# Batch norm over a matrix product on one core: the first block of w is loaded ahead of the first rows of x

## The chip, the cores and the metric

The kernel runs on one core of a Trainium2 chip. The metric is device time in microseconds, the median of several runs. Engines are named as in the profile: PE is TensorE (PEld its weight loads), DVE is VectorE, ACT is ScalarE, POOL is GpSimd, SP is SyncE. POOL and SP here also issue DMAs.

## The reference

```python
batch, m, k, n = 16, 512, 1024, 768
# x (16, 512, 1024), weight (1024, 768), float32; gamma ones, beta zeros
y = np.matmul(x, weight)
mean = np.mean(y, axis=(0, 1), keepdims=True)
var = np.var(y, axis=(0, 1), keepdims=True)
y_norm = (y - mean) / np.sqrt(var + eps)
return (gamma * y_norm + beta).astype(np.float32)
```

The product has 8192 rows and 768 columns. Mean and variance of each column go over all 8192 rows, so nothing can be stored before the last row has been multiplied.

## The kernel before

x is worked through in 16 chunks of 512 rows. The loads convert x and w to bfloat16 on the way into SBUF. x is needed with its k index across the partitions, so every landed piece of x goes through a transpose on DVE (L413, L420) before PE can use it; w needs nothing more. The k index is cut into four blocks called jw, each of 256 values: `w_sb[:, jw]` is one block of w, and a product of 512 rows and 128 columns sums over jw = 0 to 3 and two halves e.

**Loads.** `load_x` (L385) issues four DMAs for a piece of x, `load_w` (L377) four for one or more blocks of w, all on POOL's queue. The list `order` (L425) names the loads in turn: `("x", q)` is a piece of 256 rows, called x0, x1, x2, x3 in this text, `("w", a, b)` the blocks a to b-1 of w, called w0 for block 0, w1 for block 1, and w2 for blocks 2 and 3 together; `("c", c)` is a chunk of 512 rows and `("p", ...)` a part of the last chunk. POOL's queue has at most eight loads out at one time: each further one waits for the one issued eight before it. Ahead of all this SP reads one element of each of 128 rows of w into the tile `touched` (L341 to L344), which nothing uses afterwards.

**PE's start.** `wake` (L569) issues products of zeros into a bank nobody reads: first WAKE = 8 of 512 columns in float32 and SMALL = 22 small ones, and later FILL = 2 more of the large ones (L764). Then come the first chunk's products. `part(0, 1, [0])` is x0 with block 0 of w (four products L492 for the first 256 columns, eight L557 for the other 512), `part(1, 2, [0])` is x1 with block 0, `part(0, 2, [1])` both with block 1, and the rest takes blocks 2 and 3. After that each chunk of 512 rows is multiplied with the first 256 columns (L492, through `rows_unit`) and, for the first chunks, with the other columns (L557, through `col_unit`).

**What sets the order.** The kernel is written as tasks with an engine, a cost, dependencies and a priority. `arrange` (L122) plays them through with modelled times and writes down the order in which each engine issues them; each engine then runs its list strictly in that order, waiting on semaphores for data. The FILL task depends in the plan on w0's load alone:

```python
part(0, 1, [0])
fill_slot = Slot(banks)
pe_task(0.87 * FILL, wake(FILL, fill_slot), [w_ready[0]], takes=[fill_slot])
part(1, 2, [0])
part(0, 2, [1])
```

On the chip it waits for nothing of w. All products write into a ring of eight PSUM banks (`psum`), FILL among them.

The tail of the kernel (normalising and storing, L920 onwards, and L1279 to L1295 for the last columns) isn't touched.

Of the kernel before, what the change touches and what calls it, by code (L numbers as in the profile page):

```python
# [227 lines left out]
def kernel(  # L228
# [9 lines left out]
    nc = tc.nc  # L238
    f32 = mybir.dt.float32
# [8 lines left out]
    P = 128  # L248
# [9 lines left out]
    WAKE = 8  # L258
    FILL = 2
    SMALL = 22  # L260
    EARLY = 4
    SHORT = 2
    GA = 2
# [5 lines left out]
    RC = C - 2  # L269
    XT, YB, SQ = C - EARLY, 27, 3  # L270
    ADDED = (0,6,16,28,40)
# [10 lines left out]
    singles = ctx.enter_context(tc.tile_pool(name="singles", bufs=1))  # L282
# [7 lines left out]
    def seq(bi):  # L290

        ins = bi.ins
        prev = last.get(ins.engine)
        if prev is not None:
            tc.add_manual_dep(
                ins, prev,
                mybir.DependencyInfo(mybir.DependencyClass.NoSync, mybir.DependencyReason.DATA),
                reason="order",
            )
        last[ins.engine] = ins.name  # L300
        return bi
# [36 lines left out]
    warm = singles.tile([P, 1], f32)  # L338

    seq(nc.scalar.activation(warm, eps_sb, AF.Sqrt))  # L340
    touched = singles.tile([P, 1], f32)  # L341
    first_rows = weight.rearrange("(i jw c e) n -> i jw c (e n)", i=4, jw=JW, e=2)
    for i in range(4):
        seq(nc.sync.dma_start(touched[32 * i:32 * i + 32], first_rows[i, 0, :, 0:1]))  # L344


    tasks, turns = [], {}
# [11 lines left out]
    def act(occ):  # L359
        return {"ACT": (occ, occ + 0.11)}  # L360
# [61 lines left out]

    for c in range(C):
        x_slot[c] = Slot(xts)
    order = [("x", 0), ("w", 0, 1), ("x", 1), ("w", 1, 2), ("w", 2, 4)]  # L425
    order += [("x", q) for q in range(2, SHORT * QPC)] + [("c", c) for c in range(SHORT, C - 1)]
    at = M - CH
    for rows in (CH-P,P):
# [81 lines left out]
    def part_chunk(c, now, engines, small=False, step=0.0, after=()):  # L510

        src = x_slot[c]
        slots = [Slot(sqs if jw < SQ else ys) for jw in range(JW)] if small else [Slot(xts)] * JW
        ts = []

        def copy(jw):
            def emit(eng):
                if small:
                    if jw < SQ:
                        x_pl = sqpool.tile([P, 2, CH], bf16, tag="sq")  # L520
                    else:
                        x_pl = ypool.tile([P, 2, CH], bf16, tag="y")
                    slots[jw].tile = [x_pl]
                elif jw == 0:
                    x_pl = xtpool.tile([P, JW, 2, CH], bf16, tag="xT")
                    slots[0].tile = [x_pl[:, i] for i in range(JW)]
                dst = slots[jw].tile[0 if small else jw]
                pairs = src.tile[:, jw].rearrange("p m e -> p e m")
                seq(nc.scalar.copy(dst, pairs) if eng == "ACT" else ENG[eng].tensor_copy(dst, pairs))  # L529
            return emit  # L530

        for jw in range(JW):
            new = small or jw == 0
            ts.append(task(
                now + step * jw, engines, copy(jw), [x_ready[c, q, JW] for q in range(QPC)] + list(after) + ([] if new else ts[:1]),
                len(engines) > 1, uses=[src] + ([] if new else [slots[jw]]), takes=[slots[jw]] if new else []))
        plain[c] = slots, ts, small
# [31 lines left out]
    def wake(count, slot):  # L569
        def emit(eng):  # L570
# [3 lines left out]
            small = idle_sb[:, 0:P // 2].bitcast(bf16)  # L574
            for _ in range(SMALL if count == WAKE else 0):
                seq(nc.tensor.matmul(idle_ps[:, 0:P], small, small, start=True, stop=True))  # L576
# [244 lines left out]
    for c in range(1, RC):  # L821
        for ts in ([0, 1], [2, 3]):
            rows_unit(c, ts)
        if c in PARTED:
            part_chunk(c, clock[0] + (4.0 if c < EARLY else 20.0), act(1.05))
        columns = ([c - 1] if 0 < c - 1 < EARLY and c - 1 in PARTED else []) + (
            [c] if c < EARLY and c not in PARTED else [])
        for c1 in columns:
# [372 lines left out]
    STEP = {2: 1.9, 3: 2.3, 4: 2.3}  # L1201
    CHUNKS = {nt: list(range(EARLY, C)) for nt in range(GA, NT)}
    if LATE:
        late = [c for c in range(EARLY, C) if c in LATE or c + 1 - c % 2 * 2 in LATE]
        rest = [c for c in range(EARLY, C) if c not in late]
# [97 lines left out]
    order = arrange(tasks, turns)  # L1303
# [39 lines left out]
```

## Time and profile before

| | |
|---|---|
| median of 5 runs | 208.31 us (207.90 to 208.97) |
| the profiled execution | 208.15 us |
| its span, first to last instruction | 206.3 us |
| mean granted TensorE clock over the span | 0.979 |
| HBM read, written | 36.71 MB, 25.17 MB |
| loads on POOL's queue | 64.9% of the 16 DMA engines' span |

The span is what the profile's rows are measured in; 1.85 us of the execution lie outside it. The table in slices divides the span into 40 parts of 5.16 us. In the timeline a row gives start, length, engine, line, operation, the tile written and the tile read, the number of instructions merged in it, and in brackets the idle time of that engine before it and who ended it. In the chain of waits a row gives start, length, engine and line of the work that the end of the kernel depended on. A DMA's row shows its issue on POOL, not its transfer; the time from the start of an issue to its landing comes from the view of one source line.

### The profile page before, as it was taken

The page shows a single profiled execution, that of the slowest core. Times are in us where ns is not written, and L with a number is a line of the kernel's source. Part 1 is how long each engine was busy: PE and PEld are TensorE (multiplying, and loading weights), DVE is VectorE, ACT ScalarE, POOL GpSimd, SP SyncE. Part 2 cuts the span into 40 slices and gives each one's busy share as a digit, 9 for nine tenths or more (in the row PEclk, how much of TensorE's full clock was granted, in tenths as well). Part 3 has the DMA queues.
Part 4 walks back from the last instruction along what each step waited for, and adds up shares of the span by engine and source line. Part 5 has one row for each costly group of instructions (what it writes and reads, how often), then busy time and mean ns, then how long its engine had stood idle before and what let it go on. Part 6 is the DMA issues. An engine that isn't in the chain of part 4 may idle for free.

```text
span 206.3 us, 3516 instructions
## 1 busy us (share of the span) xinstructions
PE 192.5 (93%) x1226; PEld 117.9 (57%) x1226; DVE 156.4 (76%) x238; ACT 139.2 (67%) x248; POOL 131.7 (64%) x148
## 2 busy tenths in 40 slices
PE   7999999999999999999999999999999999996900
PEld 3467564747488888777865444444444445464900
DVE  4220879999999999968979998878999649666900
ACT  2000560369979999998859767997476777685960
POOL 7987954878498999998304998599945440800000
PEclk9999999999999999999999999999999999999695
DMA  5999999999999999999576998999999999999898
GB/s 60 173 185 192 195 196 196 199 194 196 191 193 196 197 197 196 196 197 194 93 99 205 330 341 300 259 354 275 321 301 250 302 299 314 313 344 347 254 347 255
DMA packets 98497, 48.73 MB, mean 236 GB/s; under 512 B 24240, under 2 KB 97968, under 8 KB 98480
## 3 DMA queue, kind: packets, MB, share of 16 engines
q0 software_dynamic: 34688, 18.36, 64.9%
q1 hardware_dynamic: 63792, 30.16, 53.9%
q8 instruction: 9, 0.15, 0.3%
q14 instruction: 8, 0.07, 0.1%
HBM read 36.71 MB, written 25.17 MB: 300 GB/s over the span
## 4 chain that ended last, share of the span: by engine, by line
PE 86%; ACT 6%; DMA 2%; DVE 1%; ACTq 0%; issue 0%
PE y_ps L557 52%; PE y_ps L492 24%; PE idle_ps L573 6%; ACT o_sb L1292 3%; PE o_ps L1027 2%; DMA r_sb<-y_sb 2%; PE a_ps L886 1%; ACT x_pl L529 1%; PE y_ps L735 1%; ACT y_sb L702 1%; PE idle_ps L576 1%; ACT y_ps L706 1%; ACT y_sb L810 1%; PE o_ps L1057 0%; ACT y_sb L654 0%; ACTq L1338 0%
## 5 line engine op out<-in xcount | busy, mean ns | idle before, releaser
L557 PEld LDWEIGHTS <-w_sb 128*128 128x128 bf16 x512 | 49.6, 97 | 57.3
L557 PE MATMUL y_ps<-x_pl,w_sb 128*128 128x512 bf16 x264 | 60.5, 379 | 0.0
L557 PE MATMUL y_ps<-xT_sb,w_sb 128*128 128x512 bf16 (+1 forms) x248 | 55.9, 377 | 0.0
L391 POOL DMA_DIRECT2D ring<-in_x_dram x76 | 47.5, 630 | 12.6 <-DVE xT_sb L413 4.9
L492 PE MATMUL y_ps<-w_sb,xT_sb 128*128 128x256 bf16 x448 | 50.6, 273 | 0.0
L492 PEld LDWEIGHTS <-xT_sb 128*128 128x128 bf16 x448 | 43.7, 98 | 7.3 <-issue 0.6
L420 DVE STREAM_TRANSPOSE xT_sb<-ring 128x1024 f32<-128x1024 f32 (+1 forms) x29 | 31.2, 1111 | 11.6 <-DMA ring<-in_x_dram 11.4
L693 DVE BATCH_NORM_STATS2 stats<-y_ps 128x6 f32<-128x512 f32 x46 | 30.7, 687 | 11.0 <-PE y_ps L557 10.9
L697 ACT CAST y_sb<-y_ps 128x512 bf16<-128x512 f32 x51 | 29.1, 591 | 13.1 <-DVE stats L693 11.4
L925 POOL TENSOR_TENSOR ring<-ring,sum 128x1024 f32<-128x1024 f32 (+1 forms) x11 | 23.7, 2182 | 14.8 <-DVE ring L920 14.8
L648 POOL TENSOR_TENSOR sum<-sum,sq_sb 128x512 f32<-128x512 f32 x21 | 26.9, 1280 | 3.3 <-ACT sq_sb L641 2.1
L641 ACT ACTIVATE sq_sb<-y_ps 128x512 f32<-128x512 f32 x28 | 16.3, 607 | 17.7 <-PE y_ps L492 17.2
L644 DVE TENSOR_TENSOR sum<-y_ps,sum 128x512 f32<-128x512 f32 x28 | 18.9, 675 | 9.2 <-ACT sq_sb L641 8.0
L529 ACT COPY x_pl<-xT_sb 128x1024 bf16<-128x1024 bf16 x24 | 24.4, 1051 | 1.7 <-DVE xT_sb L420 1.7
L529 POOL COPY x_pl<-xT_sb 128x1024 bf16<-128x1024 bf16 x15 | 16.1, 1109 | 8.0 <-DVE x_pl L529 5.2
L654 ACT CAST y_sb<-y_ps 128x512 bf16<-128x512 f32 x28 | 15.9, 600 | 7.7 <-DVE sum L644 7.4
L1192 ACT CAST ring<-ring 128x1024 f32<-128x1024 bf16 x15 | 15.7, 1048 | 2.7 <-DMA ring<-y_sb 2.5
L920 DVE TENSOR_TENSOR ring<-y_sb,a_ps 128x1024 f32<-128x1024 bf16 (+1 forms) x16 | 16.7, 1080 | 0.6 <-DMA out_dram<-ring 0.6
L1138 POOL TENSOR_TENSOR ring<-ring,sum 128x1024 f32<-128x1024 f32 x4 | 9.4, 2355 | 8.0 <-DVE ring L1134 8.0
L1027 PE MATMUL o_ps<-ident,y_sb 128*128 128x128 bf16 x104 | 11.9, 247 | 2.0 <-DVE y_sb L1279 2.0
L413 DVE STREAM_TRANSPOSE xT_sb<-ring 128x2048 bf16<-128x2048 bf16 x6 | 13.5, 2289 | 0.2 <-DMA ring<-in_x_dram 0.2
L573 PE MATMUL idle_ps<-idle_sb 128*128 128x512 f32 x20 | 11.5, 735 | 1.5 <-DVE idle_sb L313 1.5
(97 smaller groups left out, 156.2 us busy)
## 6 DMA issues: line engine op xcount, KB each, us to landing
out_dram<-ring SPq DMA_DIRECT2D x38, 512.0 KB, 4.0
ring<-in_x_dram POOLq DMA_DIRECT2D x52, 256.0 KB, 8.9
out_dram<-o_sb SPq DMA_DIRECT2D x6, 512.0 KB, 4.4
ring<-in_x_dram POOLq DMA_DIRECT2D x16, 128.0 KB, 5.2
out_dram<-ring SPq DMA_DIRECT2D x4, 256.0 KB, 2.7
w_sb<-in_weight_dram POOLq DMA_DIRECT2D x8, 96.0 KB, 4.5
w_sb<-in_weight_dram POOLq DMA_DIRECT2D x4, 192.0 KB, 5.3
ring<-in_x_dram POOLq DMA_DIRECT2D x4, 192.0 KB, 8.2
```

The source lines that it names most:

```text
L391: bi = seq(nc.gpsimd.dma_start(x_bf[32 * i:32 * i + 32], src[:, :, KQ * i:KQ * (i + 1)]))
L420: seq(nc.vector.transpose(dst, src[:, :, jw0:jw1]))
L492: seq(nc.tensor.matmul(y_ps[:, s], x_of(c, jw, e, t * P, (t + 1) * P), w_sb[:, jw, e, 0:NA], start=(s == 0 and jw == 0 and e == 0), stop=( ...
L529: seq(nc.scalar.copy(dst, pairs) if eng == "ACT" else ENG[eng].tensor_copy(dst, pairs))
L557: seq(nc.tensor.matmul(y_ps, w_sb[:, jw, e, nt * P:(nt + 1) * P], moving(c, jw, e, q0 * QR, q1 * QR, parted), start=(jw == 0 and e == 0 an ...
L573: seq(nc.tensor.matmul(idle_ps, idle_sb[:, 0:P], idle_sb, start=True, stop=True))
L644: seq(nc.vector.tensor_add(sum1, slot.tile[:, 0:n], sum1))
L648: seq(ENG[eng].tensor_add(acc, acc, state["sq"][:, 0:n]))
L693: seq(nc.vector.bn_stats(dst, slot.tile))
L697: seq(nc.scalar.copy(y(nt, c), slot.tile))
L920: seq(nc.vector.tensor_mul(slot.o, y_row[c].y[:, s0:s1], aff[0][:, None, :].to_broadcast([P, n, NA])))
L925: seq(ENG[eng].tensor_add(slot.o, slot.o, row[:, None, :].to_broadcast([P, n, NA])))
```

## The change

In the list `order`, `("w", 0, 1)` is put ahead of `("x", 0)`; the rest of the list stays. The length of the SP reads gets a name, TOUCH, with the value that stood there, 1.

```diff
@@ -258,6 +258,7 @@
+    TOUCH = 1
@@ -338,10 +339,10 @@
-    touched = singles.tile([P, 1], f32)
+    touched = singles.tile([P, TOUCH], f32)
     first_rows = weight.rearrange("(i jw c e) n -> i jw c (e n)", i=4, jw=JW, e=2)
     for i in range(4):
-        seq(nc.sync.dma_start(touched[32 * i:32 * i + 32], first_rows[i, 0, :, 0:1]))
+        seq(nc.sync.dma_start(touched[32 * i:32 * i + 32], first_rows[i, 0, :, 0:TOUCH]))
@@ -422,7 +423,7 @@
-    order = [("x", 0), ("w", 0, 1), ("x", 1), ("w", 1, 2), ("w", 2, 4)]
+    order = [("w", 0, 1), ("x", 0)] + [("x", 1), ("w", 1, 2), ("w", 2, 4)]
```

Two engines' instruction lists differ from before. POOL issues the four loads of w0 and then the four of x0, where it was the other way round. On PE the two idle products of FILL stand ahead of the first chunk's first products, where they stood between x0's and x1's products with block 0. DVE, ACT and SP issue the same instructions in the same order; DVE's first transpose still waits for x0.

## The prediction

> **What bounds the kernel now.** I read the page first (shares, then the slices), then TensorE's waits, then the chain of waits in order of time, then the timeline of the first 28 us on all engines, because the change touches only what is loaded there.
>
> ```profile
> PE 192.5 (93%) x1226; PEld 117.9 (57%) x1226; DVE 156.4 (76%) x238; ACT 139.2 (67%) x248; POOL 131.7 (64%) x148
> ...
> PE   7999999999999999999999999999999999996900
> ...
> DMA  5999999999999999999576998999999999999898
> ```
>
> TensorE is busy for 93% of the span, and in the first half the DMA engines are as full as it is. So a load that comes late has nowhere to hide unless TensorE doesn't need it yet. TensorE's own waits, all of the execution:
>
> ```profile
> PE o_ps L1027 <- DVE y_sb L1279: 2.0, 1, 2.0
> PE idle_ps L573 <- DVE idle_sb L313: 1.5, 1, 1.5
> PE a_ps L886 <- ACT y_sb L810: 0.2, 1, 0.2
> ```
>
> The columns are total, times and longest. It idles at the start, in the tail, and for 0.2 us in the middle; no wait names a load. The chain of waits (start, length) says what fills the start:
>
> ```profile
> 1.49 9.67 PE idle_ps L573 x16
> 11.16 1.23 PE idle_ps L576 x22
> 12.39 0.44 PE y_ps L492 x4
> 12.82 0.91 PE y_ps L557 x8
> 13.73 1.72 PE idle_ps L573 x4
> 15.45 0.44 PE y_ps L492 x4
> ...
> 19.47 1.75 PE y_ps L492 x16
> ...
> 24.83 3.57 PE y_ps L492 x32
> ...
> 35.63 3.49 PE y_ps L492 x32
> ```
>
> Until 12.39 TensorE multiplies idle data (L573, L576), and does so again from 13.73 to 15.45. From there real products follow one another. The row at 24.83 is the one to keep: its 32 products took 3.57 us where the same 32 at 35.63 took 3.49. The timeline shows why, and where the loads are issued:
>
> ```profile
> 1.30 2.44 POOL L391 DMA_DIRECT2D ring<-in_x_dram  x4 [0.86 <-POOLq L1324]
> ...
> 3.74 1.99 POOL L382 DMA_DIRECT2D w_sb<-in_weight_dram  x4
> ...
> 8.07 1.30 DVE L420 STREAM_TRANSPOSE xT_sb<-ring 128x512 f32<-128x512 f32 x2 [4.94 <-DMA ring<-in_x_dram]
> 8.23 0.58 POOL L391 DMA_DIRECT2D ring<-in_x_dram  x1 [0.30 <-DMA ring<-in_x_dram]
> ...
> 12.89 1.30 DVE L420 STREAM_TRANSPOSE xT_sb<-ring 128x512 f32<-128x512 f32 x2 [3.52 <-DMA ring<-in_x_dram]
> ...
> 25.18 1.25 DVE L420 STREAM_TRANSPOSE xT_sb<-ring 128x1024 f32<-128x1024 f32 x1 [0.54 <-DMA ring<-in_x_dram]
> ...
> 26.48 1.64 PEld L492 LDWEIGHTS <-xT_sb 128*128 128x128 bf16 x16 [0.18 <-DVE xT_sb L420]
> ```
>
> The fourth block of x rows (x3) lands at 25.04, VectorE turns it from 25.18 to 26.43, and TensorE's weight loads had already waited 0.18 us for that. Here the load stream has no reserve: what it loses before 25 us, TensorE loses, from here to the end. What it gains is worth at most 3.57 - 3.49 = 0.08 us.
>
> **The change, part by part.**
>
> *The issues.* POOL issues the same eight DMAs, w first. Before: four of x in 2.44 us, four of w in 1.99, done at 5.73. After: the same eight durations (577 to 583 ns for x, 492 to 510 for w, some 150 ns extra on whichever is first), so 4.43 us again and done at 5.73. Difference 0. SP's queue keeps its order, and ACT's and DVE's as well.
>
> *w0's landing.* The last of its issues starts near 2.95. Issue to landing was 3.4, 3.6, 3.7 and 4.8 us for the first four DMAs of the kernel before. With the longest of these, w0 is there at 7.75, against 5.24 + 4.6 = 9.85 before. TensorE doesn't come to it until 14.1 (below), so those 2 us are worth 0.
>
> *x0's landing.* Its last issue starts near 5.15. By w0's rows (4.6 to 4.7 in that place) it lands at 9.8, by x0's own slowest row (4.8) at 9.95; before it was 8.0. VectorE's pair of transposes (1.30) then runs to 11.25. VectorE has nothing else there: it idled until 8.07 and again until 12.89. So 0, with the reserve in the next step; without VectorE's idle time it would cost up to 1.30.
>
> *TensorE's order.* The instruction lists differ in one place: the two idle products of FILL (the 1.72 us row, 4 passes) now stand ahead of the first real block, since in the plan they come free when w0 has landed and x0 is now later. So TensorE runs idle products to 12.39 + 1.72 = 14.11, then both halves of the first block back to back: 0.44 + 0.91 + 0.44 + 0.91. Before: 0.44 + 0.91 + 1.72 and the second half from 15.45. The second half starts at 12.39 + 3.07 = 15.45 in both; 0. x0 is needed at 14.11 and turned at 11.25, a reserve of 2.9 us; if x0 came later than that, each further microsecond would be paid. x1 (turned at 14.19, needed at 15.45) keeps 1.26. The bank of FILL is now taken five tiles earlier, so the ring of eight banks turns differently for the next tiles; the bank that is freed later than before is wanted again by the tile at 35.63, and ScalarE emptied the last column block of the first rows at 27.04 + 1.78 = 28.8. Worth 0.
>
> *POOL behind it.* At most eight POOL loads are out at a time, so the fourth load of x1 waited 0.30 us (row at 8.23) for x0's fourth. After, it waits for w0's fourth, there at 7.75 at the latest, and that wait goes. The next, w1's, then wait for x0's four (the last at 9.8 to 9.95 where the issue before stood at 10.35), so none is later. Gain between 0 and 0.30 us of issue time; since x1 and w1 took 4.4 to 4.7 us from issue to landing against 3.4 for an unloaded one, they mostly stood behind other transfers, and I take 0.
>
> *The stream itself.* This is the unknown: does the stream move as fast when w's transfers stand first? Call its shift at x3 d. In half-microsecond stretches it moved 57, 149, 161, 191, 178 GB/s from 3.0, then 121, 149, 138 from 5.5 to 7.0, against a mean of 191 from 9.85 to 25. The dip lacks (70 + 42 + 53) x 0.5 us = 82 KB, or 0.43 us. If the order x-then-w makes that dip, it may vanish: d = -0.43. On the other side, x0's fourth load landed 1.7 us behind its third where its transfer takes 131 KB / 191 = 0.69: 1.0 us late. If a first read of w now pays that as well (SP's four small reads of w, issued from 0.74 to 2.5, landed only by 2.1 + 2.8 = 4.9, while w0's bytes will now move from about 3.1), d = +1.0. Bytes, issues and packets are the same, so I take d = 0, nearest to the x1-to-w1 change of source at 11.5 to 13.0, which ran at 182 to 191 GB/s with no dip.
>
> The Trainium skill speaks on how much reserve x3 has. Its page "DMA: Bandwidth & Descriptors", section "Anatomy of one DMA — SWDGE (gpsimd) path", puts such a DMA at 2.0 us plus bytes over 436 GB/s, which for the 262 KB read is 2.6 us, an estimate. By it x3's last load (issued at 18.84) would land at 21.4 and any d up to 3.6 us would cost nothing; the row has 6.2 us and a landing at 25.04, so I go by the row, where d > 0 is paid in full.
>
> *Other needs.* w1's last landed at 14.7 and is used at 16.79; w2's last landed at 18.55 and is used at 19.47, so 0.92 in reserve: x3 decides first.
>
> *The sum.* 208.15 (this execution: span 206.3 and 1.85 around it) + issues 0 + order 0 + the shift: max(-0.08, d) = 0, so 208.15. The median of the five runs is 208.31, 0.16 above, and the changed kernel will be judged by such a median: 208.3. Ends: at most 0.08 + the 0.2 at a_ps L886 below, 1.0 above.
>
> **The rivals.**
>
> *A, no change (the forecast).* For it: no wait of TensorE names a load; both halves fit at 15.45. Against it: x3 has no reserve. 208.3, its own range 207.9 to 208.8.
>
> *B, slower: w's first read is slow, and x3 pays.* Place: x3's transpose at 25.18. Price: d, up to 1.0, so 208.3 + 1.0 = 209.3. It decides from d = 0.62 on, which is 0.3% of the time and about what a measurement of this kernel can tell from no change. For it: SP's third and fourth small reads took 2.5 and 2.8 us against 1.5 for the first. Against it: no later meeting with w showed a comparable loss, 13.5 to 14.0 at 135 GB/s being the worst (0.15 us).
>
> *C, faster: the early dip goes and the front of the kernel comes forward.* 0.43 for the dip and 0.22 for the wait at a_ps: 0.65, so 207.65. For it: VectorE waits for x at 25.18 (0.54). Against it: TensorE shows only 0.08 to gain there.
>
> *D, the edit doesn't do what it says.* TOUCH is 1, which is what stood there, so that part does nothing, and the first product comes 1.7 us later rather than earlier. The time is A's.
>
> **How the numbers follow.** A and D together 0.68, B 0.22, C 0.10. A and D leave 0.03 of scatter on the fast side and 0.05 on the slow side. B gives 0.20 slower and 0.02 same, C 0.07 faster and 0.03 same. So faster 0.10, same 0.65, slower 0.25. The range 207.6 to 209.1 takes in C's time and most of B's.
>
> **What would show it.** Right: first real product near 14.1, the second half of the first block near 15.45 and no idle TensorE between; x3's transpose at 25.2 within 0.3 and the granted clock 1.00 throughout the first 26 us. B: x3's transpose at 25.8 or later with a wait on VectorE in TensorE's list. C: x3 before 24.9. Wrong altogether: x0 turned after 14.1, or a time that moves while TensorE stands at 24.83 as before.

## The result and the profile after

The changed kernel is slower: a median of 209.49 us over 49 runs against 208.70 us over 91 runs of the kernel before, taken beside it. The ratio is 1.0029, with a 95% interval of 1.0017 to 1.0042, so about 0.6 us; the two medians differ by 0.79. The kernel before had shown 208.31 in its first five runs. Of the 1.2 us between the forecast of 208.3 and the median measured, 0.39 is that, and the rest the change. The profiled execution took 209.33 us, its span is 207.5 (206.3 before).

The page of the changed kernel, the lines that answer to those of before (lines of code are one higher):

```profile
PE 192.7 (93%) x1226; PEld 116.4 (56%) x1226; DVE 156.8 (76%) x238; ACT 138.9 (67%) x248; POOL 131.7 (63%) x148
...
DMA  4999999999999999999686899999999999999898
```

TensorE's busy time is the same within 0.2 us, 192.7 against 192.5 before. What has changed is when it may begin. Its waits, whole execution, in the same columns as before; the waits at the start (1.5) and in the tail (2.0) are as they were, and stand ahead of these rows:

```profile
...
PE y_ps L493 <- DMA w_sb<-in_weight_dram: 0.6, 1, 0.6
PE y_ps L493 <- DVE xT_sb L421: 0.4, 1, 0.4
PE a_ps L887 <- ACT y_sb L811: 0.3, 1, 0.3
```

The first two are new: TensorE now waits for a load of w and for a transpose of x. The timeline of the start shows where:

```profile
1.26 2.13 POOL L383 DMA_DIRECT2D w_sb<-in_weight_dram  x4 [0.81 <-POOLq L1325]
...
3.38 2.33 POOL L392 DMA_DIRECT2D ring<-in_x_dram  x4
...
8.39 0.58 POOL L392 DMA_DIRECT2D ring<-in_x_dram  x1 [0.49 <-DMA w_sb<-in_weight_dram]
...
10.94 1.31 DVE L421 STREAM_TRANSPOSE xT_sb<-ring 128x512 f32<-128x512 f32 x2 [7.80 <-DMA ring<-in_x_dram]
...
13.98 0.60 PE L493 MATMUL y_ps<-w_sb,xT_sb 128*128 128x256 bf16 x4
...
15.32 0.60 PE L493 MATMUL y_ps<-w_sb,xT_sb 128*128 128x256 bf16 x4
...
20.14 1.91 PE L493 MATMUL y_ps<-w_sb,xT_sb 128*128 128x256 bf16 x16 [0.63 <-DMA w_sb<-in_weight_dram]
...
26.49 1.25 DVE L421 STREAM_TRANSPOSE xT_sb<-ring 128x1024 f32<-128x1024 f32 x1 [0.94 <-DMA ring<-in_x_dram]
...
27.79 1.38 PE L493 MATMUL y_ps<-w_sb,xT_sb 128*128 128x256 bf16 x11 [0.38 <-DVE xT_sb L421]
```

Up to 15.32 TensorE is on its old schedule (15.29 before). Then it has stood still for 0.63 us when w2 lets it go on at 20.14, and for 0.38 us when x3 does at 27.79, whose transpose starts at 26.49 where it stood at 25.18. From there the delay is carried along. The chain of waits has the row of the third chunk at 36.94 (35.63 before), and far behind it a row that before stood at

```profile
173.35 1.08 PE y_ps L557 x5
```

and now here:

```profile
36.94 3.49 PE y_ps L493 x32
...
174.76 1.08 PE y_ps L558 x5
```

So the loss, 1.3 us at the third chunk and 1.4 at the later row, is made between 15 and 28 us and nothing gives it back. What makes the loads late is seen in a table by stretches. Its columns are: the stretch, its length, busy time of PE, PEld, DVE, ACT and POOL, the granted clock, the DMA engines' share, and the GB/s moved. The kernel before:

```profile
3.00:4.50 1.50, 1.50 (x3) 0.62 (x2) 0.14 (x3) 0.00 (x0) 1.50 (x4) 1.00 1.10 122
4.50:6.00 1.50, 1.50 (x3) 0.47 (x3) 0.00 (x0) 0.00 (x0) 1.50 (x5) 1.00 1.31 163
6.00:8.00 2.00, 2.00 (x6) 0.83 (x5) 0.00 (x0) 0.30 (x1) 1.86 (x4) 1.00 1.14 168
8.00:10.00 2.00, 2.00 (x6) 0.94 (x5) 1.30 (x2) 0.00 (x0) 1.76 (x4) 1.00 1.24 188
10.00:12.00 2.00, 2.00 (x21) 1.29 (x20) 0.00 (x0) 0.00 (x0) 1.87 (x4) 1.00 1.41 187
12.00:15.00 3.00, 3.00 (x23) 2.07 (x21) 1.30 (x2) 0.00 (x0) 2.48 (x5) 1.00 1.03 184
```

The changed kernel:

```profile
2.50:3.00 0.50, 0.50 (x2) 0.34 (x1) 0.44 (x2) 0.00 (x0) 0.50 (x2) 1.00 0.50 49
3.00:4.50 1.50, 1.50 (x3) 0.63 (x2) 0.14 (x3) 0.00 (x0) 1.50 (x3) 1.00 1.14 160
4.50:6.00 1.50, 1.50 (x3) 0.47 (x3) 0.00 (x0) 0.00 (x0) 1.50 (x5) 1.00 0.80 85
6.00:8.00 2.00, 2.00 (x6) 0.85 (x5) 0.00 (x0) 0.30 (x1) 1.81 (x4) 1.00 1.12 132
8.00:10.00 2.00, 2.00 (x6) 0.92 (x5) 0.00 (x0) 0.00 (x0) 1.37 (x3) 1.00 1.32 161
10.00:12.00 2.00, 2.00 (x22) 1.31 (x21) 1.06 (x2) 0.00 (x0) 1.20 (x3) 1.00 1.02 106
12.00:15.00 3.00, 3.00 (x21) 1.82 (x19) 0.79 (x2) 0.00 (x0) 1.99 (x4) 1.00 1.27 205
```

Compare the last column. The stream begins better (49 from 2.5, where the kernel before moved nothing yet, then 160 against 122), then has two holes: 85 against 163 GB/s from 4.5 to 6.0, and 106 against 187 from 10 to 12. Each difference times its stretch, divided by the 191 GB/s of the full stream, is time gained or lost: +0.30, -0.61, -0.38, -0.28, -0.85, +0.33, and +0.13 for the first bytes. The sum up to 15 us is -1.36 us, about the 1.31 by which x3's transpose is later; from 15 to 25 us the two streams differ little (193 GB/s before, 189 after). The clock stays at 1.00 throughout.

### The profile page after: what moved, and what is told of

The parts are those of the page before. It is cut to its first block, busy times and chain, and to the rows that moved or that the text cites. A ratio compares the mean times of both kernels' runs of the same rounds, so it can differ in the third digit from the quotient of the medians.

```text
span 207.5 us, 3516 instructions
## 1 busy us (share of the span) xinstructions
PE 192.7 (93%) x1226; PEld 116.4 (56%) x1226; DVE 156.8 (76%) x238; ACT 138.9 (67%) x248; POOL 131.7 (63%) x148
## 4 chain that ended last, share of the span: by engine, by line
PE 73%; DMA 11%; ACT 7%; POOL 3%; DVE 1%; issue 1%; ACTq 0%; DVEq 0%; POOLq 0%
PE y_ps L558 48%; PE y_ps L493 21%; DMA ring<-in_x_dram 6%; ACT o_sb L1293 3%; DMA w_sb<-in_weight_dram 3%; DMA r_sb<-y_sb 2%; POOL w_sb L383 2%; PE o_ps L1028 2%; POOL ring L392 1%; PE a_ps L887 1%; ACT x_pl L530 1%; PE y_ps L736 1%; ACT y_sb L703 1%; ACT y_ps L707 1%; DVE xT_sb L421 1%
## 5 line engine op out<-in xcount | busy, mean ns | idle before, releaser
L694 DVE BATCH_NORM_STATS2 stats<-y_ps 128x6 f32<-128x512 f32 x46 | 30.7, 687 | 10.8 <-PE y_ps L558 10.7
L698 ACT CAST y_sb<-y_ps 128x512 bf16<-128x512 f32 x51 | 29.2, 590 | 12.6 <-DVE stats L694 10.9
L645 DVE TENSOR_TENSOR sum<-y_ps,sum 128x512 f32<-128x512 f32 x28 | 18.9, 675 | 8.5 <-ACT sq_sb L642 7.2
L1193 ACT CAST ring<-ring 128x1024 f32<-128x1024 bf16 x15 | 15.7, 1048 | 3.4 <-DMA ring<-y_sb 3.3
L1028 PE MATMUL o_ps<-ident,y_sb 128*128 128x128 bf16 x104 | 11.8, 221 | 2.1 <-DVE y_sb L1280 2.0
```

Source lines behind the costliest of these rows:

```text
L645: seq(nc.vector.tensor_add(sum1, slot.tile[:, 0:n], sum1))
L694: seq(nc.vector.bn_stats(dst, slot.tile))
L698: seq(nc.scalar.copy(y(nt, c), slot.tile))
```

## The experiments

Landings and waits in a table row are those of one profile, in us from the span's start; the ratio comes from several runs and is to the kernel before, run beside it. "Eight" is when the last of the first eight loads (x0 and w0) landed, "w2" its last piece, "x3" the start of its transpose. The waits are TensorE's: first for w2, then for x3 (in e6 for x1, in e7 and f3 for x1 and x3 together).

| run | eight | w2 | x3 | waits | ratio, interval |
|---|---|---|---|---|---|
| before | 9.9 | 18.6 | 25.18 | none | |
| after | 10.8 | 20.0 | 26.49 | 0.63, 0.38 | 1.0029 (1.0017 to 1.0042) |
| a1 | 10.9 | 19.8 | 25.78 | 0.72, 0 | 1.0033 (1.0004 to 1.0061) |
| e1 | 9.8 | 18.4 | 25.02 | 0, 0.38 | 1.0000 (0.9978 to 1.0023) |
| e2 | 11.1 | 20.2 | 26.25 | 0.9, 0 | 1.0182 (1.0154 to 1.0210) |
| e4 | 10.5 | 18.8 | 25.38 | none | 1.0039 (1.0018 to 1.0060) |
| e5 | 10.7 | 19.1 | 26.13 | 0, 0.56 | 1.0041 (1.0009 to 1.0074) |
| e6 | 10.6 | 20.0 | 25.91 | 1.05, 0.60 | 1.0043 (1.0014 to 1.0072) |
| e7 | 12.1 | 20.9 | 27.67 | 1.13, 1.06 | 1.0183 (1.0134 to 1.0232) |
| e8 | 9.7 | 19.4 | 25.07 | 0.63, 0 | 0.9991 (0.9959 to 1.0023) |
| f1 | 10.1 | 19.3 | 25.32 | none | 1.0557 (1.0497 to 1.0618) |
| f2 | 10.3 | 19.6 | 26.21 | 0.66, 0.53 | 1.0631 (1.0576 to 1.0687) |
| f3 | 11.8 | 21.2 | 27.60 | 1.42, 0.83 | 1.0609 (1.0560 to 1.0657) |
| f4 | 9.9 | 18.4 | 24.80 | 0, 0.32 | 1.0593 (1.0529 to 1.0657) |
| g1 | 10.2 | 18.8 | 25.18 | 0.56, 0.32 | 1.0542 (1.0492 to 1.0592) |
| g2 | 9.6 | 18.9 | 25.37 | 0, 0.37 | 1.0552 (1.0503 to 1.0601) |
| g3 | 10.7 | 19.6 | 26.13 | 0.62, 0.44 | 1.0619 (1.0574 to 1.0664) |
| g4 | 10.4 | 19.4 | 25.57 | none | 1.0564 (1.0520 to 1.0608) |

**a1, the changed kernel again.** No edit.

> The changed kernel once more, beside the kernel before on the same chip. If the late load stream is a property of the change, x3's transpose stands near 26.5 us again (26.49 in the first profile, 25.18 before), TensorE waits 0.6 us for w2 and 0.4 us for x3, and the time is 0.2 to 0.6% over before. If the first profile was an accident of one execution, x3's transpose is back near 25.2 and the time is that of before.

The time and the wait for w2 came again. x3 was late by 0.6 rather than 1.3 us: one profile is one draw, and scatters by some half microsecond.

**e1, TensorE's order alone.**

```diff
-    pe_task(0.87 * FILL, wake(FILL, fill_slot), [w_ready[0]], takes=[fill_slot])
+    pe_task(0.87 * FILL, wake(FILL, fill_slot), [], takes=[fill_slot])
```

> The kernel before with only TensorE's order of the change: FILL ahead of the first block, loads as they were. If the loads' order is the cause, x3's transpose stays near 25.2 and the time within 0.2% of before. If the moved idle products (or the banks behind them) cost the time, it is 0.3% slower with the loads where they were.

The time of before, within 0.2% to each side. The moved idle products and their bank cost nothing that this shows, and less than the 0.3% of the change.

**e2 and e5, w first without SP's small reads.** e2 drops reads and tile, e5 keeps the tile.

```diff
     for i in range(4):
-        seq(nc.sync.dma_start(touched[32 * i:32 * i + 32], first_rows[i, 0, :, 0:TOUCH]))
+    seq(nc.vector.memset(touched, 0.0))
```

> The changed kernel without SP's four small reads of w. Theory cold: w's first read is slow in any place, and the small reads had warmed the first two pieces (2.8 and 2.7 us to landing) but came too late for the other two (4.1 and 5.2). Then without them all four pieces of w0 take 4 us or more, x3's transpose comes at 26.5 or later, and the time is 0.3 to 1% over before. Theory collision: the small reads, still under way until 4.7 us, held up w0's third and fourth piece. Then all four land within 3.5 us, x3 is back near 25.2 to 25.5 and the time near that of before.

> The changed kernel without SP's four reads of w, but with the tile they went to still in its place (VectorE sets it to zero), so that no later tile moves by 4 bytes. In the run without reads and tile, w0's pieces landed at 4.0, 4.4, 6.0 and 6.6 us, as with the reads, and the stores of the tail took 2 us longer. If the reads of w are idle and the tile's 4 bytes were what cost the tail, the time is that of the changed kernel, 0.2 to 0.6% over before, and the tail after TensorE is 10 us again. If the reads matter to something in the tail, it stays near 1.8% over before.

w0's pieces landed at 4.0, 4.4, 6.1 and 6.6 (e2) and 4.0, 4.5, 5.7 and 6.5 (e5); with the reads it was 4.1, 4.6, 6.5, 8.1 (after) and 4.1, 4.6, 6.1, 6.6 (a1). So neither expectation of e2 came: the reads neither help w0 nor hold it up when w goes first, and e5's time is the changed kernel's within the intervals. e2's 1.8% is another matter. Its tail, from the first transpose of TensorE's last block to the end, takes 18.3 us (192.19 to 210.5) against 15.7 (e5) and 15.6 (before), and the large stores from o_sb take 5.9 us to land against 4.7 and 4.4. e2 and e5 differ by the 4-byte tile and its setting to zero early on. What that leaves as the cause is the place of the tiles behind it, which no run here varied by itself.

**e4, the reads from two queues.** SP issues two, ACT two ahead of its table load.

```diff
-    seq(nc.scalar.activation(warm, eps_sb, AF.Sqrt))
 ...
-        seq(nc.sync.dma_start(touched[32 * i:32 * i + 32], first_rows[i, 0, :, 0:TOUCH]))
+        seq((nc.sync, nc.scalar)[i // 2].dma_start(touched[32 * i:32 * i + 32], first_rows[i, 0, :, 0:TOUCH]))
+    seq(nc.scalar.activation(warm, eps_sb, AF.Sqrt))
```

> The changed kernel with the four small reads issued two by SP and two by ACT, so that all are out by about 1.6 us instead of 2.5. Theory cold: the third and fourth read return a microsecond sooner, w0's third and fourth piece land in 3 to 3.5 us instead of 4.1 and 5.2, x3's transpose comes 0.5 to 1.3 us earlier than 26.5 and the time falls back by 0.1 to 0.3%. Theory collision: the same reads still meet w0's first pieces, and x3 stays at 26.2 or later. If x's own first read is what stretches the stream, w0 is quick and x3 is late all the same.

The last reads had landed by 3.0 us instead of 4.8, and w0's third and fourth piece took 3.6 us all the same, as in a1 (3.6 and 3.7); the median stayed up. The profile is a quick execution (208.13 us of its own, no wait for a load), so it doesn't stand for the median.

**e6, the kernel before without the reads.** The edit of e5 on the kernel before.

> The kernel before without SP's four reads of w (tile kept, set to zero by VectorE). Theory cold w: w0, now the first reader of w, lands 0.5 us or more after 9.85, x3's transpose comes after 25.5 and the time is 0.1 to 0.4% over before. Theory that w isn't what is slow: w0 lands at 9.8, x3 at 25.2 and the time is that of before within 0.2%.

Here the reads do matter: without them the time is 0.43% up (0.14 to 0.72). In the profile the eight land 0.7 us later and x3 is turned at 25.91; the profiles with the reads, in this order, range to 10.4 and 25.57 (g4). So in the old order the reads are worth about as much as the old order itself.

**e7, an early read of x.** One element of each of x0's rows, on ACT's queue.

```diff
+    xtouched = singles.tile([P, 16], f32)
+    for i in range(2):
+        seq(nc.scalar.dma_start(
+            xtouched[64 * i:64 * i + 64, 0:2],
+            x_flat[128 * i:128 * i + 128, 0:1].rearrange("(p a) k -> p (a k)", a=2)))
```

> The changed kernel with one element of each of x0's 256 rows read by ACT's queue at about 0.8 us, ahead of the loads. Theory cold x: with x first, the slow first reads of x lie in the start, where nothing else could move; with w first they lie in the middle of the stream. Then, read early, x0's pieces land a microsecond or more before 8.8 to 10.8, x3's transpose is back below 25.6 and the time within 0.2% of before. If x's first reads are not what is slow, x0 lands at 8.8 to 10.8 again and the time stays 0.2 to 0.6% over before.

Cold x falls in this form: x0 landed later, not sooner (8.9 to 12.1, after 8.8 to 10.8). The time is not to be read against the others: here too o_sb's large stores take 5.9 us, as in e2, and here too a tile ahead of the later ones has changed.

**e8, an idle operation on POOL.**

```diff
+    seq(nc.gpsimd.memset(tot, 0.0))
```

> The kernel before with one idle operation on POOL ahead of its first load (it sets a tile to zero that is written again much later), which puts every early load back by its length, some 0.5 to 1 us, with nothing else changed. Theory of the late stream: TensorE has no reserve at x3, so a stream that is late by d costs TensorE d there (less 0 to 0.1), a wait on VectorE of that length appears, and the time rises by about d, 0.2 to 0.5%. If the stream's lateness is not what costs the time, the waits appear but the time moves by less than 0.1%, or no waits appear.

It says nothing on the question: its 0.53 us fitted into a wait that POOL has anyway, the first load moved from 1.30 to 1.33, and the time stayed. What it does show is the scatter: this profile waits 0.63 us for w2, as the changed kernel's does, and has 207.2 of span, in a kernel that is as fast as before. (TensorE's other wait for a transpose, 0.42 us, stands at 81.41 and isn't x3's.)

**f1 to f6, g1 to g4: another form.** In these TensorE turns y everywhere, and no DMA does. The first 95 us are the same instructions in the same order; the later part is longer. The code that this leaves unused goes as well.

```diff
-    MODE = {2:'xact',3:'xact',4:('pe',)*2+('xact',)*1+('pe',)*5}
+    MODE = {2:'pe',3:'pe',4:'pe'}
-    RAW, RAWADD, RAWDUE = {2:(0,2),4:(0,2)}, {2:'POOL',3:'POOL',4:'POOL'}, {2:14.0,3:8.0,4:8.0}
+    RAW, RAWADD, RAWDUE = {}, {2:'POOL',3:'POOL',4:'POOL'}, {2:14.0,3:8.0,4:8.0}
```

> The kernel before in another form, the base for the next runs: y is turned by TensorE everywhere, where the kernel before turns part of it by DMA; the first 95 us are the same instructions in the same order. Its time may be some per cent longer, which is of no interest; x3's transpose should stand at 25.0 to 25.3 us and TensorE wait 0 to 0.6 us for w2 and x3 together.

The base: 220.18 us, x3 at 25.32.

> The change, put into that form. If its cost lies in the first 30 us, it is there again: x3's transpose at 25.4 to 26.5, TensorE's waits for w2 and x3 0.5 us or more above the base's, and the time 0.3 to 0.9 us above the base's. If the cost came from the transposes by DMA behind the loads, the two times are the same.

222.73 us, and again 221.61 against 220.51 in g3 and g4: by the medians 2.55 and 1.1 us above the base, by the ratios 1.5 and 1.1. TensorE's waits of f2 (f1 has none for a load):

```profile
PE y_ps L493 <- DMA w_sb<-in_weight_dram: 0.7, 1, 0.7
PE y_ps L493 <- DVE xT_sb L421: 0.5, 1, 0.5
```

The intervals overlap in both pairs, so the times alone settle neither size nor sign. The chains of waits do better. The same row near 148 us, in f1, f2, g4 and g3:

```profile
147.61 1.74 PE y_ps L557 x8
...
148.28 1.74 PE y_ps L558 x8
...
147.68 1.69 PE y_ps L557 x7
...
148.25 1.69 PE y_ps L558 x7
```

With w first it stands 0.67 and 0.57 us later, about the 0.6 that the change costs in its own kernel, and no transpose by DMA has a part in it. The spans differ by more, 2.2 and 2.0 us. The rest arises behind this row: from 150 to 160 us f2 and g3 ran at a granted clock of 0.83, f1 and g4 at 1.00. The profile of g1 has 0.83 there as well, and its median is not above the base's. Why the clock falls there in some executions, and whether the order of the loads has a part in it, no run here shows. The stretch in f1, then in f2 (the clock is the third column from the right):

```profile
150.00:160.00 10.00, 7.85 (x56) 4.12 (x55) 8.43 (x13) 5.09 (x8) 6.86 (x7) 1.00 0.41 124
...
150.00:160.00 10.00, 7.85 (x43) 3.77 (x41) 7.73 (x11) 4.24 (x8) 7.47 (x8) 0.83 0.35 106
```

**f3, the old order with a late stream.** Three idle operations on POOL.

```diff
+    for _ in range(3):
+        seq(nc.gpsimd.memset(tot, 0.0))
```

> The base with three idle operations of POOL ahead of its first load (one alone fitted into POOL's own wait at the start and moved the first load by only 0.03 us). The first load now starts 1.0 us later, and so does the stream. Theory of the late stream: TensorE waits 0.5 to 1.0 us more than in the base for w2 and x3, and the time rises by 0.5 to 1.0 us. If a late stream is made up for later, the waits are there but the time moves by less than 0.3 us.

The first load starts at 2.62 instead of 1.30 (1.3 us, not 1.0). x3's transpose comes 2.3 us later than in f1, and the time is 1.55 us up by the medians (1.1 by the ratios, whose intervals overlap), the span 1.8. TensorE's waits for loads:

```profile
PE y_ps L494 <- DMA w_sb<-in_weight_dram: 1.4, 1, 1.4
PE y_ps L494 <- DVE xT_sb L422: 0.8, 2, 0.5
```

A late stream, made late by nothing but its start, brings the same waits for w2 and x3 (0.29 of the 0.8 us; the other 0.54 is for x1), and the delay is kept: the row near 148 us stands at 149.66, 2.05 us behind f1's, at a clock of 1.00 in both.

**f4, all of w read beforehand.**

```diff
+    for jw in range(1, JW):
+        for i in range(4):
+            seq(nc.sync.dma_start(fin[32 * i:32 * i + 32, jw:jw + 1], first_rows[i, jw, :, 0:1]))
```

> The base with twelve more small reads on SP, of the blocks w1 to w3, so that all of w has been read once before its loads. Theory cold w: the slow packets of w1 and w2 between 11.5 and 14.5 us vanish, w2's last piece lands 0.3 us or more before 18.5 and x3 before 25.0; TensorE gains at most the 0.1 to 0.4 us that it waits there, so 0 to 0.4 us. If small reads themselves disturb the stream, w0 and x1 land later and the time rises by 0.2 us or more.

w2 lands 0.9 us and x3's transpose comes 0.5 us sooner than in f1 (but w2 hardly sooner than in e1, at 18.4 without them), and the packets between 12 and 15 us are hardly slow any more: the time that they took beyond their usual 248 ns (w) and 60 ns (x) sums to 0.6 us over all engines, against 5.2 in f1. The row near 148 us stands at 146.87, 0.74 us ahead of f1's; in the time no gain shows (220.7 against 220.18, intervals of 1.3 us to each side).

**f5 and f6, w first with a lead for the reads.** The change on the base, with eight of f3's idle operations ahead of the loads; f6 also without the reads.

> The base with the change and with eight idle operations of POOL (0.53 us each) ahead of its loads, so that SP's four reads of w have landed (by 4.9 us) before w0's first bytes move. Only the stream from the first load on is of interest; TensorE will wait some 3 us and the time rise by that. Theory cold w: w0's third and fourth piece now land 2.7 us after their issue like the first two (3.6 to 5.2 with the loads at once). Theory that the third and fourth piece at any start of the queue are slow: 3.6 us or more again.

> The run before this one, without the four reads of w (tile kept). Theory cold w: w0's third and fourth piece take 3.3 us or more, as in the changed kernel. Theory that something else in the first 8 us of an execution slows transfers, whatever they carry: now that the loads start behind it, all four pieces take 2.7 us although w wasn't read.

One run each, 227.54 and 226.43 us. w0's four pieces took 2.7, 2.6, 3.6, 3.6 us from issue to landing with reads that had all landed by 3.7 us, the loads starting at 5.5; and 2.7, 2.7, 2.7, 3.7 without reads. Cold w falls as the reason for w0's slow half: a lead doesn't mend it. The first 8 us of an execution aren't it either: w's packets took 338 and 363 ns on average from 6.5 to 7.5 us (248 is usual) and x's 72 and 70 ns from 9 to 15 us (60 is usual). Nor is a first read of w slow by itself: in g3, below, the 384 packets of w1 and w2, which nothing had read before in that execution, took 248 ns at most.

**g1 and g2, x and w in turns.** g1 issues one piece of x0, w0's four, and the rest of x0; g2 w and x by turns. The dependencies stay the base's. Only the loop of `load_x` is shown; `load_w` is changed so that it issues the pieces named to it.

```diff
-            for i in range(4):
+            for i, ws in enumerate(((), (0, 1, 2, 3), (), ()) if m0 == 0 else ((),) * 4):
+                if ws:
+                    load_w(0, 1)(eng, ws)
                 bi = seq(nc.gpsimd.dma_start(x_bf[32 * i:32 * i + 32], src[:, :, KQ * i:KQ * (i + 1)]))
```

> The base with the first eight loads in the order: one piece of x0, the four of w0, the other three of x0. Theory queue start (what is loaded first pays, and w pays more than x): with one piece of x ahead w0's pieces come at full speed, all eight have landed by 10.1 us as in the base, x3's transpose stands at 25.0 to 25.4 and the time is the base's within 0.5 us. Theory x last (x behind w lands late whatever is at the start): the eight have landed only by 10.5 to 11, x3 is at 25.8 or later and the time 0.6 us or more above the base.

> The base with the first eight loads in turn, w0, x0, w0, x0 and so on, w0's first piece at the head. Theory queue start: only the one piece of w at the head pays; all eight by 10.0 to 10.4, x3 at 25.2 to 25.6, time within 0.7 us of the base. Theory x last: the last of x0 stands last here too, so 10.5 or later, x3 at 25.8 or later and 0.6 us or more above the base.

> The base with the change once more, on the same chip as the two before: all eight landed by 10.3 to 10.9, x3's transpose at 25.8 to 26.5, TensorE's waits for w2 and x3 1 us or more, the time 0.6 to 2.5 us above the base.

> The base once more, on the same chip: all eight landed by 9.7 to 10.1, x3's transpose at 25.0 to 25.4, TensorE's waits for w2 and x3 under 0.6 us together.

219.86 and 220.1 us against 220.51 of the base and 221.61 of the change, x3 at 25.18 and 25.37 against 25.57 and 26.13. "x last" falls: x0's last piece stands last in both, and neither is slow. The stretch of the first hole in g1, and then in g3:

```profile
4.50:6.00 1.50, 1.50 (x5) 0.57 (x4) 0.00 (x0) 0.00 (x0) 1.50 (x5) 1.00 1.02 182
```

```profile
4.50:6.00 1.50, 1.50 (x3) 0.53 (x3) 0.00 (x0) 0.00 (x0) 1.50 (x5) 1.00 0.74 110
```

One piece of x at the head fills the first hole (182 against 110 GB/s). It doesn't spare all waits: TensorE's list in g1 has 0.56 us for w2 and 0.32 for x3, where g4's has none, though the row near 148 us stands at 147.29 in g1 and 147.50 in g2, ahead of the base's 147.68. So the list of waits alone is not the delay. The DMA packets in the trace say what the hole is:

```
                     w0: first, 96th, last of 128 packets    x: first, 1024th
before               6.43   8.53   9.53                      3.15   7.61
changed              2.63   5.28   7.79                      5.41   9.62
g3 (w first)         2.62   5.28   6.06                      5.51   9.40
g1 (one x first)     3.87   6.04   7.52                      2.80   8.95
```

(start of the first, end of the others, in us from the span's start; x0 has 1024 packets). With w first, three quarters of w0 have gone through by 5.28, and x0's first packet comes only at 5.41, 2.0 us after its issue began at 3.38; the engines' share falls to 0.80. Before, x0 was still moving when w0's first packet came, for 7.61 - 6.43 = 1.2 us. The hole is thus shown; that it comes from w's short pieces running out before x's first bytes can follow is read off these numbers and not proved.

## Why the prediction was wrong

*The issues, TensorE's order, the bank* were right. POOL finished the eight issues at 5.71 (5.73 was forecast), the first real product came at 13.98 (14.11) and the second half at 15.32 (15.45) with no gap (the timeline, from which these are, had 15.29 where the chain of before has 15.45); e1 priced this order at 0.

*The landings.* w0's last came at 8.1 in the first profile, where 7.75 was the latest allowed, but at 6.4 to 6.6 in the other six with w first. x0's was forecast too early: at 9.95 at the latest, and it came at 10.8, at 10.3 to 11.1 over the seven. It was read from w0 behind x0, where the two overlapped by 1.2 us; behind w0 no such overlap came.

*POOL behind it* was right in one half. The 0.30 us wait became 0.49 in the first profile, but in the other six it went, as forecast (x1's fourth issue at 7.9 instead of 8.23). The issues of w1 were to be no later, and were: the last at 11.09 instead of 10.3, at 10.6 to 11.4 over the seven, since at most eight loads are out and x0's came back late.

*"Other needs"* named x3 as the first to decide. It was w2 that bound first: 0.92 in reserve, and 1.45 later in the first profile (20.01 against 18.56).

*The stream* is the step that failed: "Bytes, issues and packets are the same, so I take d = 0". d was 1.31 in the first profile. Over the seven profiles with w first (after, a1, e2, e4, e5, f2, g3), x3's transpose stands at 26.05 on average, over the six with x first and the reads (before, e1, e8, f1, f4, g4) at 25.16: d = 0.9. TensorE's waits for w2 and x3 average 0.78 against 0.22 us, a difference of 0.56, beside the 0.6 that the ratio gives and the 0.57 and 0.67 of the rows near 148 us. The row I chose, the change from x1 to w1 in a full stream, says nothing of an empty one. That x3 has no reserve and d is paid was right in the main, and f3 shows it by another way: 2.3 us of lateness at x3, 2.05 kept at 149.66. The Trainium skill's fit ("DMA: Bandwidth & Descriptors", "Anatomy of one DMA — SWDGE (gpsimd) path"), 2.6 us by the prediction's estimate, is not what this trace shows for x3's last load: 6.1 us from issue to landing in the changed kernel, 6.2 before.

*The rivals.* A fell with d = 0. B had the place, nearly the price (1.0 for d), and the sign, but by luck: its cause, w's cold first read, fell with e5, f5 and the packets of w1 and w2 in g3. The range ended at 209.1 and cut off B's upper part, and the base moved up by 0.39. C fell: the front went back, not forward. In D the later first product (13.98, 12.22 before, by the timeline) is as it says; its time, A's, fell.

*Open*: why w0's third and fourth piece mostly take 3.3 to 5.2 us where the first two take 2.7; the second hole at 10 to 12 us, in which x's packets were slow (77 ns on average, 63 before); and why the reads help when x goes first (e6) and not when w does. g1's order was not tried on the kernel before with its transposes by DMA; its 0.65 us below the base is inside the intervals.

## What to carry to other kernels

A reorder of loads that keeps bytes and issues can still leave a hole in the stream: look at its first microseconds for what keeps it fed while the next load's first bytes are under way. One piece of x at the head filled that hole here (g1); that it pays against the old order isn't shown. Judge the price not at the loads that moved but at the next consumer without reserve. Take more than one profile before giving a microsecond at the start a cause. And where two times differ by more than the change can explain, compare the chains row by row: in f2 and g3 the larger part of the difference in span was made 120 us later, at another clock.

## What was not expected of the hardware

Between the start of an issue and its first packet lay 1.4 us for w at the head, 1.5 to 1.9 for x at the head, and 1.7 to 2.4 for x behind w. Four small reads of w (one element of each of 128 rows) are worth 0.43% when w is loaded 3 us after them (e6) and nothing measurable right behind them (e5). And without a tile of 4 bytes for each partition the tail was 2.6 us longer, the large stores landing in 5.9 instead of 4.7 us (e2 against e5).
